# A unit's seventh product behind the next unit's second, rotary tables by residue, and angles once per token and frequency

## The chip, the core and the metric

One core of a Trainium2 chip runs the whole kernel. The metric is the device time in microseconds (us). Engines: TensorE (PE) multiplies, VectorE (DVE) and ScalarE (ACT) work on tiles in SBUF and on the accumulators in PSUM, GpSimd (POOL) on tiles in SBUF, and SyncE (SP) issues all DMAs. Each engine runs its own list of instructions in order. An instruction that waits holds back everything behind it on its engine.

## What is computed

The reference, cut to what the change touches. `h` is the normalised input, 1024 tokens by 1024 features; all is float32.

```python
z = h @ w_in[l]                        # 7696 columns; 1536 of them d_q, 1536 d_k
gates = jax.nn.sigmoid(h @ w_gate[l] + b_gate[l])          # 3072 columns

def rope(x, pos):                      # on d_q and d_k, head size 128
    inv = ROPE_THETA ** (-jnp.arange(0, hd, 2, dtype=jnp.float32) / hd)
    ang = pos.astype(jnp.float32)[..., None] * inv         # 64 frequencies
    cos = jnp.cos(ang)[:, :, None, None, :]
    sin = jnp.sin(ang)[:, :, None, None, :]
    x1, x2 = xf[..., :hd // 2], xf[..., hd // 2:]
    return jnp.concatenate([x1 * cos - x2 * sin, x2 * cos + x1 * sin], axis=-1)
# then three groups of heads attend with dilation 1, 4 and 16: the tokens of one
# residue modulo the dilation make a sequence of their own
```

## The kernel before

**Units.** The projections by `w_in` and `w_gate` are done in units of 256 output columns by 1024 tokens, each a call of `seven`. Channels lie on the partitions, tokens along the free axis. A unit's result is 2x2 blocks of 128x512, and seven block products give it instead of eight. Every float32 operand is split in a high and a low part (`split`: an ACT copy, line 160, and a DVE subtraction, line 161), so a product is four contraction blocks times three matmuls, 12 matmuls of 128x128 by 512. A unit has 84. A unit has three PSUM accumulators. In PE order the products go to X, Y, Z, X, Z, X and X; here they are called product 1 to 7. ACT copies products 1, 3 and 4 out of PSUM (lines 316, 321, 324), DVE adds products 2, 5 and 6 to those copies (lines 318, 327, 329). Products 4, 6 and 7 go on accumulating in X and product 5 in Z, so product 5 cannot begin before line 321 has read Z, product 6 not before line 324 has read X, and product 7 not before line 329 has read X.

**Product 7** is put off: `seven` leaves it in `pending`, and the next unit calls `last_product()` right behind its own product 1 (line 314). Its result, block (1,0), is handed to `use` in PSUM.

**Operands.** A unit's seven weight operands lie in two sets of tiles, operands 1 to 4 in the first and 5 to 7 in the second. The same two sets serve the next unit: its operands 1 to 4 can be written when product 4 is done, its operands 5 to 7 when product 7 is done. The raw weights come by two DMAs of 512 KB into a pool of three `raw` buffers. POOL makes the sums of weight blocks (lines 293 to 299).

**Rotary units.** Between 233 us and 675 us run 22 units: one gate unit (columns 8 and 9 of `w_gate`), 12 rotary ones (`rope_out`: d_q and d_k in turn, four per dilation) mixed with 7 further gate units, and two of `gla_out`. Written T and L (light, a gate unit), the mix is L T L T T L T T L T L T T L T T L T T. For each of its four blocks a rotary unit has ACT copy the two halves of the partitions crosswise into `sw` (lines 519, 520), DVE multiply the block by the cosine (line 526), POOL multiply `sw` by the sine (line 527), and DVE add (line 528). The result is sent to `d_qk` by a DMA. For dilations 4 and 16 lines 526 and 528 read by `perm`, with a stride of 4 or 16 elements, and write the tokens in order of residues.

**Angles.** Lines 488 to 509 make the tables `cos` and `sin`, 128 partitions by 1024 tokens. The 64 frequencies stand twice on the partitions. 16 DVE instructions reduce the angle to -pi to pi, three ACT instructions take the sine.

**Order.** The code is written in the order of the units. A list scheduler lays out each engine's list at compile time, with semaphores for every dependence.

Of the kernel before, what the change touches and what calls it, by code (L numbers as in the profile page):

```python
# [9 lines left out]
F32 = mybir.dt.float32  # L10
F32R = mybir.dt.float32r
I32 = mybir.dt.int32
U8 = mybir.dt.uint8
AF = mybir.ActivationFunctionType
OP = mybir.AluOpType

T = 1024
# [55 lines left out]
def trunk(ctx: ExitStack, tc, x, positions, w_in, w_alpha_up, b_alpha, gla_norm_g, sc_conv_w,  # L73
          w_gate, b_gate, w_branch, w_mix_out, pre_mix_g, post_mix_g, pre_ffn_g, post_ffn_g,
          w_ff_gate, w_ff_up, ff_conv_w, ff_conv_b, w_ff_down, const, masks, out):
    nc = tc.nc
    V, S, G, PE = nc.vector, nc.scalar, nc.gpsimd, nc.tensor

    main = ctx.enter_context(tc.tile_pool(name="main", bufs=1))
    rawp = ctx.enter_context(tc.tile_pool(name="raw", bufs=3))  # L80
# [5 lines left out]
    def pt(tag, name):  # L86
        return psum.tile([128, 512], F32, name=name, tag=tag,
                         bufs={"g": 4, "s": 2, "t": 1, "o": 1}[tag])
# [176 lines left out]
            split(*out(2), f12)  # L265
            split(*out(3), t4)

    def seven(src, c0, B, Ts, tmp, dst, use):


        v = src.rearrange("(k p) c -> p k c", p=128)
        r0, r1 = wload([v[:, :4, c0:c0 + 256], v[:, 4:, c0:c0 + 256]], [8, 256])
# [7 lines left out]
        op = lambda i: ops[i]  # L280
# [25 lines left out]
        def prod(ps, a, b, first):  # L306
            for k in range(4):
                for n, (x, y) in enumerate(((0, 0), (0, 1), (1, 0))):
                    PE.matmul(ps, a[x][:, k], b[y][:, k], start=first and k == 0 and n == 0,  # L309
                              stop=k == 3 and n == 2, skip_group_check=not first)  # L310

        X, Y, Z = pt("g", "sX"), pt("s", "sY"), pt("g", "sZ")
        prod(X, op(0), blk(0, 0), True)
        last_product()
        c11 = dst(0, 0)
        S.activation(c11, X, AF.Copy)
        prod(Y, op(1), blk(1, 0), True)
        sums_taken[1] = V.tensor_tensor(c11, c11, Y, op=OP.add)
        prod(Z, op(2), tt(0), True)
        c22 = dst(1, 1)  # L320
        sums_taken[2] = S.activation(c22, Z, AF.Copy)
        prod(X, op(3), tt(1), False)
        c12 = dst(0, 1)
        sums_taken[3] = S.activation(c12, X, AF.Copy)
        use(0, 0, c11)
        prod(Z, op(4), blk(1, 1), False)
        sums_taken[4] = V.tensor_tensor(c12, c12, Z, op=OP.add)
        prod(X, op(5), tt(2), False)
        sums_taken[5] = V.tensor_tensor(c22, c22, X, op=OP.add)  # L329
        use(0, 1, c12)  # L330
        use(1, 1, c22)

# [3 lines left out]
        pending.append(rest)  # L336


    pending = []

    sops, sums_taken = [], {}

    def op_places():

        ts = [[wp.tile([128, 4, 4, 128], F32R, name=n, tag=n) for n in ("wh", "wl")] for i in range(2)]
        return Ring([(h[:, i], l[:, i]) for h, l in ts for i in range(4)])

    def last_product():
        while pending:
            pending.pop(0)()  # L350
# [134 lines left out]
    last_product()  # L485


    cos, sin = fr[:, 0], fr[:, 1]
    pos = rawp.tile([128, T], I32, name="pos", tag="raw")
    nc.sync.dma_start(pos, bass.AP(tensor=positions.tensor, offset=positions.offset, ap=[[0, 128], [1, T]]))  # L490
    ang, nn = cos, sin
    V.tensor_scalar(ang, pos, cst[:, K_INV:K_INV + 1], None, op0=OP.mult)
    MAGIC = 1.5 * 2.0 ** 23
    V.tensor_scalar(nn, ang, 1.0 / (2.0 * math.pi), MAGIC, op0=OP.mult, op1=OP.add)
# [6 lines left out]
    V.tensor_scalar(nn, ang, -PI, 2.0 * math.pi, op0=OP.is_lt, op1=OP.mult)  # L501
    V.tensor_tensor(ang, ang, nn, op=OP.add)
    V.tensor_scalar(ang, ang, 3.1415925, -3.1415925, op0=OP.min, op1=OP.max)
    ac = fr[:, 2]
    V.scalar_tensor_tensor(ac, ang, -1.0, ang, op0=OP.mult, op1=OP.max)
    V.tensor_scalar(ac, ac, -1.0, math.pi / 2.0, op0=OP.mult, op1=OP.add)
    S.activation(sin[:64], ang[:64], AF.Sin, scale=-1.0)
    S.activation(sin[64:], ang[64:], AF.Sin)
    S.activation(cos, ac, AF.Sin)
    seven(w_gate2, 8 * 128, H, TS, STMP, ring, gate_out(8))  # L510

    DIL = (1, 4, 16)
    SW = Ring([fr[:, 2, :512], fr[:, 2, 512:]])

    def rope_out(w, ch):
        def use(i, l, c):
            hs = slice(l * 512, l * 512 + 512)
            sw = SW()
            S.activation(sw[:64], c[64:], AF.Copy)
            S.activation(sw[64:], c[:64], AF.Copy)  # L520

            d = DIL[ch // 512]
            perm = (lambda x: x) if d == 1 else (lambda x: x.rearrange("p (m r) -> p r m", r=d))
            as_ = (lambda x: x) if d == 1 else (lambda x: x.rearrange("p (r m) -> p r m", r=d))
            o = c if d == 1 and (i, l) != (1, 0) else ring()
            V.tensor_tensor(as_(o), perm(cos[:, hs]), perm(c), op=OP.mult)
            G.tensor_tensor(sw, sw, sin[:, hs], op=OP.mult)  # L527
            V.tensor_tensor(as_(o), as_(o), perm(sw), op=OP.add)  # L528
            r = ch + i * 128
            nc.sync.dma_start(d_qk[w, r:r + 128, hs], o)  # L530
        return use
# [10 lines left out]

    turned = [(w_in2, col + ch, rope_out(w, ch)) for ch in range(0, 1536, 256) for w, col in enumerate((COL_DQ, COL_DK))]
    light = [(w_gate2, dt * 128, gate_out(dt)) for dt in range(10, 24, 2)]
    nt, n = len(turned), len(turned) + len(light)
    for i in range(n):
        take = turned if (i + 1) * nt // n > i * nt // n else light
        src, c0, use = take.pop(0)
        seven(src, c0, H, TS, STMP, ring, use)
    seven(w_in2, COL_GQ, H, TS, STMP, ring, gla_out(0))  # L550
    seven(w_in2, COL_GK, H, TS, STMP, ring, gla_out(1))

# [836 lines left out]
        forms(0, ys, il)  # L1389

    sops.append(op_places())
    sums_taken.clear()
    ring = halves_ring(("t2", "t0", "t1"))
    yring = Ring([fb[:, i] for i in (0, 1, 3)])
# [124 lines left out]
    n = 0  # L1519
# [73 lines left out]
```

## Time and profile before

| what | value |
|---|---|
| median of 3 runs | 1950.78 us (1946.41 to 1953.79) |
| the profiled execution | 1952.54 us, span 1950.8 us |
| PE busy | 1887.3 us of the span |
| DVE, ACT, POOL busy | 1327.7, 876.9, 730.9 us |
| mean granted TensorE clock | 0.988 |
| PE share of the chain that ended last | 77% |

The span is the time from the first to the last instruction of the profile; 1.7 us of the execution lie around it. Times in the rows below count from the span's start. A busy PE is not PE at its peak: its clock has two levels, 2.4 GHz (1.00 in a row) and 1.2 GHz (0.50).

### The profile page before, as it was taken

To read this page: it belongs to the slowest core of one execution; us is meant where nothing else is said; L and a number is where in the kernel's file an instruction comes from. 1 tells how busy PE (TensorE), PEld (TensorE's weight loads), DVE (VectorE), ACT (ScalarE), POOL (GpSimd) and SP (SyncE) were. 2 spreads that over 40 slices of the span, in tenths; PEclk is the share of its full clock that TensorE was granted. 3 is DMA by queue.
4 is the path that set the end of the run, shared out by engine and by line. 5 is a ranking of instruction groups with operands and counts; after the bars stand their busy time and mean duration, and the time that the engine had idled before them with its cause. 6 is when DMAs were issued, how large, how long until landed. Compare 5 with 4: busy or idle time off the path is not lost.

```text
span 1950.8 us, 26312 instructions
## 1 busy us (share of the span) xinstructions
PE 1887.3 (97%) x9649; PEld 1597.8 (82%) x9649; DVE 1327.7 (68%) x1971; ACT 876.9 (45%) x1626; POOL 730.9 (37%) x438
## 2 busy tenths in 40 slices
PE   6999999999999999999999899998999999999998
PEld 5988778888777899899888777886788888888886
DVE  8755675677787543566854577677777777779597
ACT  5433354454444433424546623343443444355453
POOL 4523244555454232102013451016444444526172
PEclk9999999999999999999999999999999999999999
DMA  5122322323232565312467556321323232369863
GB/s 177 66 79 73 123 88 93 123 97 119 97 116 89 184 211 181 135 44 76 127 219 210 173 191 253 108 98 60 103 87 120 96 108 87 125 216 353 275 198 123
DMA packets 192961, 268.32 MB, mean 138 GB/s; under 512 B 30785, under 2 KB 121791, under 8 KB 191808
## 3 DMA queue, kind: packets, MB, share of 16 engines
q1 hardware_dynamic: 192832, 266.64, 40.4%
q8 instruction: 76, 1.25, 0.3%
q14 instruction: 53, 0.43, 0.1%
HBM read 191.73 MB, written 74.86 MB: 137 GB/s over the span
## 4 chain that ended last, share of the span: by engine, by line
PE 77%; DVE 10%; issue 4%; POOL 3%; ACT 3%; DMA 2%; SPq 0%; DVEq 0%; ACTq 0%; POOLq 0%
PE sX L309 24%; PE sZ L309 12%; PE sY L309 6%; PE fX L1537 6%; PE fY L1537 5%; PE vX L604 4%; DVE wl L161 2%; PE vZ L604 2%; PE p L200 1%; PE p L202 1%; PE p L204 1%; PE gs L793 1%; PE mx L1291 1%; PE mx L1293 1%; PE mx L1292 1%
## 5 line engine op out<-in xcount | busy, mean ns | idle before, releaser
L161 DVE TENSOR_TENSOR wl<-raw,wh 128x512 fp32r<-128x512 f32 (+1 forms) x212 | 212.0, 1036 | 103.6 <-ACT wh L160 103.4
L309 PE MATMUL sX<-T,wh 128*128 128x512 f32 x720 | 226.8, 397 | 11.2 <-DVE ring L329 10.5
L160 ACT ACTIVATE wh<-raw 128x512 fp32r<-128x512 f32 (+1 forms) x222 | 142.1, 665 | 79.9 <-PE sX L309 41.2
L309 PEld LDWEIGHTS sX<-T,wh 128*128 128x128 f32 x720 | 136.6, 191 | 44.6 <-DVE ring L329 15.2
L309 PE MATMUL sX<-FT,wh 128*128 128x512 f32 x480 | 149.2, 392 | 3.1 <-DVE ring L329 1.6
L309 PE MATMUL sX<-T,wl 128*128 128x512 f32 x360 | 142.2, 395 | 0.0
L527 POOL TENSOR_TENSOR fr<-fr 128x512 f32<-128x512 f32 x48 | 70.5, 1468 | 148.7 <-ACT fr L520 147.3
L309 PEld LDWEIGHTS sX<-FT,wh 128*128 128x128 f32 x480 | 89.2, 188 | 25.2 <-DVE ring L329 5.4
L161 DVE TENSOR_TENSOR wl<-fr,wh 128x512 fp32r<-128x512 f32 x90 | 65.9, 754 | 63.2 <-ACT wh L160 62.5
L160 ACT ACTIVATE wh<-fr 128x512 fp32r<-128x512 f32 (+1 forms) x99 | 63.9, 665 | 70.1 <-PE sX L309 49.1
L309 PE MATMUL sX<-FT,wl 128*128 128x512 f32 x240 | 93.5, 390 | 0.0
L293 POOL TENSOR_TENSOR fr<-raw 128x512 f32<-128x512 f32 x30 | 41.2, 1374 | 121.9 <-DMA raw<-in_w_gate_dram 45.7
L161 DVE TENSOR_TENSOR ops<-rw,ops 128x512 fp32r<-128x512 f32 x72 | 67.0, 960 | 26.2 <-ACT ops L160 25.0
L299 POOL TENSOR_TENSOR raw<-raw 128x512 f32<-128x512 f32 x50 | 80.9, 1618 | 0.0
L309 PEld LDWEIGHTS sX<-T,wl 128*128 128x128 f32 x360 | 68.8, 191 | 14.7
L1358 POOL TENSOR_TENSOR fb<-fb 128x512 f32<-128x512 f32 x40 | 64.1, 1602 | 42.7 <-DVE fb L1407 31.0
L528 DVE TENSOR_TENSOR ring<-ring,fr 128x512 f32<-128x512 f32 x48 | 56.2, 1172 | 29.7 <-POOL fr L527 28.1
L309 PE MATMUL sZ<-T,wh 128*128 128x512 f32 x240 | 73.9, 389 | 0.0
L1537 PE MATMUL fX<-ops 128*128 128x512 f32 x312 | 73.2, 389 | 0.0
L1537 PEld LDWEIGHTS fX<-ops 128*128 128x128 f32 x312 | 58.6, 188 | 12.1
L297 POOL TENSOR_TENSOR fr<-raw,fr 128x512 f32<-128x512 f32 x30 | 49.7, 1656 | 48.4 <-DVE wl L161 48.4
L160 ACT ACTIVATE ops<-rw 128x512 fp32r<-128x512 f32 x72 | 43.6, 628 | 52.4 <-PE fX L1537 23.6
(550 smaller groups left out, 5596.1 us busy)
## 6 DMA issues: line engine op xcount, KB each, us to landing
rw<-in_w_ff_down_dram SPq DMA_DIRECT2D x99, 256.0 KB
raw<-in_w_in_dram SPq DMA_DIRECT2D x48, 512.0 KB
rw<-d_fa SPq DMA_DIRECT2D x77, 256.0 KB
d_fa<-fb SPq DMA_DIRECT2D x70, 256.0 KB
raw<-in_w_gate_dram SPq DMA_DIRECT2D x24, 512.0 KB
d_sig<-ring SPq DMA_DIRECT2D x48, 256.0 KB
d_qk<-ring SPq DMA_DIRECT2D x48, 256.0 KB
raw<-in_w_ff_gate_dram SPq DMA_DIRECT2D x22, 512.0 KB
```

Source lines behind the costliest of these rows:

```text
L160: S.activation(h, src, AF.Copy)
L161: eng.tensor_tensor(l, src, h.bitcast(F32), op=OP.subtract)
L200: PE.matmul(ps[h], a, xs[h][0][:, kx, :], start=st, stop=False)
L293: G.tensor_tensor(s1, A21, A22, op=OP.add)
L297: G.tensor_tensor(s1, A12, s2, op=OP.subtract)
L299: G.tensor_tensor(A21, A11, A21, op=OP.subtract)
L309: PE.matmul(ps, a[x][:, k], b[y][:, k], start=first and k == 0 and n == 0, stop=k == 3 and n == 2, skip_group_check=not first)
L527: G.tensor_tensor(sw, sw, sin[:, hs], op=OP.mult)
L528: V.tensor_tensor(as_(o), as_(o), perm(sw), op=OP.add)
L604: PE.matmul(o, b[y][:, k, ts], a[:, x, k], start=first and t % 2 == 0 and k == 0 and n == 0, stop=k == 3 and n == 2, skip_group_check=not ...
L1358: G.tensor_tensor(o, p, q, op=op)
L1537: PE.matmul(P[t], o[:, a, ts], o[:, b], start=st, stop=c + k == NCH - 1 and x == 2, skip_group_check=i not in (2, 1, 5))
```

## The change

Three parts, all in the stretch of the rotary units.

1. From the angles on (`slack` is set there and cleared ahead of the feed-forward layer) a unit calls `last_product()` behind its own product 2 instead of product 1.
2. The tables are made half as wide: frequencies times 512 tokens, the first half of the tokens on partitions 0 to 63, the second on 64 to 127. ACT takes sine and cosine in eight instructions of 64x512. The scratch lies in `fr[:, 2]`, where it lay in the tables before.
3. For dilations 4 and 16 the order by residues is made where blocks leave PSUM: the copies and additions of `seven` read PSUM with the stride and write the block in order, and so do the instructions on block (1,0) in `rope_out`. The tables are put in the same order by `tables_by`, once ahead of each dilation, in two further `raw` buffers (6 ACT instructions for dilation 4, 18 for dilation 16). Lines 526 and 528 then read without a stride, and the product with the cosine is written back in place. The mix of units is L T T L T T three times and an L.

```diff
@@ -265,7 +265,8 @@
-    def seven(src, c0, B, Ts, tmp, dst, use):
+    def seven(src, c0, B, Ts, tmp, dst, use, d=1):
...
@@ -309,24 +310,28 @@
+        perm = (lambda a: a) if d == 1 else (lambda a: a.rearrange("p (m r) -> p r m", r=d))
+        as_ = (lambda a: a) if d == 1 else (lambda a: a.rearrange("p (r m) -> p r m", r=d))
         X, Y, Z = pt("g", "sX"), pt("s", "sY"), pt("g", "sZ")
         prod(X, op(0), blk(0, 0), True)
+        if not slack:
+            last_product()
+        c11 = dst(0, 0)
+        S.activation(as_(c11), perm(X), AF.Copy)
+        prod(Y, op(1), blk(1, 0), True)
         last_product()
-        c11 = dst(0, 0)
-        S.activation(c11, X, AF.Copy)
-        prod(Y, op(1), blk(1, 0), True)
-        sums_taken[1] = V.tensor_tensor(c11, c11, Y, op=OP.add)
+        sums_taken[1] = V.tensor_tensor(as_(c11), as_(c11), perm(Y), op=OP.add)
         prod(Z, op(2), tt(0), True)
         c22 = dst(1, 1)
-        sums_taken[2] = S.activation(c22, Z, AF.Copy)
+        sums_taken[2] = S.activation(as_(c22), perm(Z), AF.Copy)
         prod(X, op(3), tt(1), False)
         c12 = dst(0, 1)
-        sums_taken[3] = S.activation(c12, X, AF.Copy)
+        sums_taken[3] = S.activation(as_(c12), perm(X), AF.Copy)
         use(0, 0, c11)
         prod(Z, op(4), blk(1, 1), False)
-        sums_taken[4] = V.tensor_tensor(c12, c12, Z, op=OP.add)
+        sums_taken[4] = V.tensor_tensor(as_(c12), as_(c12), perm(Z), op=OP.add)
         prod(X, op(5), tt(2), False)
-        sums_taken[5] = V.tensor_tensor(c22, c22, X, op=OP.add)
+        sums_taken[5] = V.tensor_tensor(as_(c22), as_(c22), perm(X), op=OP.add)
         use(0, 1, c12)
         use(1, 1, c22)
 
@@ -336,7 +341,7 @@
         pending.append(rest)
 
 
-    pending = []
+    pending, slack = [], []
 
     sops, sums_taken = [], {}
 
@@ -485,10 +490,14 @@
     last_product()
 
 
+    slack.append(True)
     cos, sin = fr[:, 0], fr[:, 1]
-    pos = rawp.tile([128, T], I32, name="pos", tag="raw")
-    nc.sync.dma_start(pos, bass.AP(tensor=positions.tensor, offset=positions.offset, ap=[[0, 128], [1, T]]))
-    ang, nn = cos, sin
+    pos = rawp.tile([128, 512], I32, name="pos", tag="raw")
+    for l in range(2):
+        nc.sync.dma_start(pos[l * 64:l * 64 + 64],
+                          bass.AP(tensor=positions.tensor, offset=positions.offset + 512 * l, ap=[[0, 64], [1, 512]]))
+    ang, nn = fr[:, 2, :512], fr[:, 2, 512:]
     V.tensor_scalar(ang, pos, cst[:, K_INV:K_INV + 1], None, op0=OP.mult)
...
@@ -501,31 +510,53 @@
...
-    ac = fr[:, 2]
+    ac = nn
     V.scalar_tensor_tensor(ac, ang, -1.0, ang, op0=OP.mult, op1=OP.max)
     V.tensor_scalar(ac, ac, -1.0, math.pi / 2.0, op0=OP.mult, op1=OP.add)
-    S.activation(sin[:64], ang[:64], AF.Sin, scale=-1.0)
-    S.activation(sin[64:], ang[64:], AF.Sin)
-    S.activation(cos, ac, AF.Sin)
+    for l in range(2):
+        ps_, hs = slice(l * 64, l * 64 + 64), slice(l * 512, l * 512 + 512)
+        S.activation(sin[:64, hs], ang[ps_], AF.Sin, scale=-1.0)
+        S.activation(sin[64:, hs], ang[ps_], AF.Sin)
+        S.activation(cos[:64, hs], ac[ps_], AF.Sin)
+        S.activation(cos[64:, hs], ac[ps_], AF.Sin)
     seven(w_gate2, 8 * 128, H, TS, STMP, ring, gate_out(8))
 
     DIL = (1, 4, 16)
     SW = Ring([fr[:, 2, :512], fr[:, 2, 512:]])
 
+    def tables_by(d, before):
+        for t in (cos, sin):
+            raw = rawp.tile([128, T], F32, name="tab", tag="raw")
+            for l in range(2):
+                hs = slice(l * 512, l * 512 + 512)
+                n, a = 512 // d, d // before
+                src = t[:, hs].rearrange("p (r0 m r1) -> p r1 r0 m", r0=before, r1=a)
+                o = raw[:, hs].rearrange("p (r1 r0 m) -> p r1 r0 m", r1=a, r0=before)
+                if before == 1:
+                    src, o = src[:, :, 0], o[:, :, 0]
+                    S.activation(o, src, AF.Copy)
+                else:
+                    for r in range(a):
+                        S.activation(o[:, r], src[:, r], AF.Copy)
+            S.activation(t, raw, AF.Copy)
     def rope_out(w, ch):
+        d = DIL[ch // 512]
         def use(i, l, c):
             hs = slice(l * 512, l * 512 + 512)
             sw = SW()
-            S.activation(sw[:64], c[64:], AF.Copy)
-            S.activation(sw[64:], c[:64], AF.Copy)
-
-            d = DIL[ch // 512]
-            perm = (lambda x: x) if d == 1 else (lambda x: x.rearrange("p (m r) -> p r m", r=d))
-            as_ = (lambda x: x) if d == 1 else (lambda x: x.rearrange("p (r m) -> p r m", r=d))
-            o = c if d == 1 and (i, l) != (1, 0) else ring()
-            V.tensor_tensor(as_(o), perm(cos[:, hs]), perm(c), op=OP.mult)
+            perm = (lambda x: x) if d == 1 or (i, l) != (1, 0) else (lambda x: x.rearrange("p (m r) -> p r m", r=d))
+            as_ = (lambda x: x) if d == 1 or (i, l) != (1, 0) else (lambda x: x.rearrange("p (r m) -> p r m", r=d))
+            S.activation(as_(sw[:64]), perm(c[64:]), AF.Copy)
+            S.activation(as_(sw[64:]), perm(c[:64]), AF.Copy)
+            o = c if (i, l) != (1, 0) else ring()
+            V.tensor_tensor(as_(o), as_(cos[:, hs]), perm(c), op=OP.mult)
             G.tensor_tensor(sw, sw, sin[:, hs], op=OP.mult)
-            V.tensor_tensor(as_(o), as_(o), perm(sw), op=OP.add)
+            V.tensor_tensor(o, o, sw, op=OP.add)
             r = ch + i * 128
             nc.sync.dma_start(d_qk[w, r:r + 128, hs], o)
         return use
@@ -542,11 +573,16 @@
 
     turned = [(w_in2, col + ch, rope_out(w, ch)) for ch in range(0, 1536, 256) for w, col in enumerate((COL_DQ, COL_DK))]
     light = [(w_gate2, dt * 128, gate_out(dt)) for dt in range(10, 24, 2)]
-    nt, n = len(turned), len(turned) + len(light)
-    for i in range(n):
-        take = turned if (i + 1) * nt // n > i * nt // n else light
+    for what in "LTTLTT" * 3 + "L":
+        take = turned if what == "T" else light
+        d = 1
+        if what == "T":
+            g = (12 - len(turned)) // 4
+            d = DIL[g]
+            if g and len(turned) % 4 == 0:
+                tables_by(d, DIL[g - 1])
         src, c0, use = take.pop(0)
-        seven(src, c0, H, TS, STMP, ring, use)
+        seven(src, c0, H, TS, STMP, ring, use, d)
     seven(w_in2, COL_GQ, H, TS, STMP, ring, gla_out(0))
     seven(w_in2, COL_GK, H, TS, STMP, ring, gla_out(1))
 
@@ -1389,6 +1425,7 @@
         forms(0, ys, il)
 
     sops.append(op_places())
+    slack.clear()
     sums_taken.clear()
     ring = halves_ring(("t2", "t0", "t1"))
     yring = Ring([fb[:, i] for i in (0, 1, 3)])
```

The order on two engines. First PE, in the first rotary unit, where product 7 of the light unit ahead of it begins: `sX` and `sY` are accumulators, `H0h`, `H0l` and `T3` what is multiplied, `wh` and `wl` the operands. Before:

```order
L309 MATMUL sX_2132<-H0h_96,wh_2110 128x512
L309 MATMUL sX_2132<-H0l_97,wh_2110 128x512
L309 MATMUL sX_2132<-H0h_96,wl_2111 128x512
L309 MATMUL sX_2005<-T3_398,wh_1985 128x512 x2
L309 MATMUL sX_2005<-T3_398,wl_1986 128x512
```

Now:

```order
L310 MATMUL sY_2139<-H0h_96,wh_2116 128x512
L310 MATMUL sY_2139<-H0l_97,wh_2116 128x512
L310 MATMUL sY_2139<-H0h_96,wl_2117 128x512
L310 MATMUL sX_2011<-T3_398,wh_1991 128x512 x2
L310 MATMUL sX_2011<-T3_398,wl_1992 128x512
```

The old unit's product 7 (`sX<-T3`) stood directly behind the new unit's product 1 (`sX<-H0h`); now the new unit's product 2 (`sY`) stands ahead of it.

ACT in the gate unit where the sines are taken, before (the unit behind the gate unit of columns 8 and 9; `ring<-sX,cols` is that gate unit's block (1,0)):

```order
L160 ACTIVATE wh<-fr 128x512
L507 ACT_TABLE_LOAD
L507 ACTIVATE fr<-fr 64x1024
L508 ACTIVATE fr<-fr 64x1024
L160 ACTIVATE wh<-raw 128x512
L509 ACTIVATE fr<-fr 128x1024
L160 ACTIVATE wh<-raw 128x512
L449 ACT_TABLE_LOAD
L449 ACTIVATE ring<-sX,cols 128x512
L321 ACTIVATE ring<-sZ 128x512
L449 ACTIVATE ring<-ring,cols 128x512
```

Now (in the gate unit of columns 8 and 9 itself):

```order
L454 ACTIVATE ring<-ring,cols 128x512
L326 ACTIVATE ring<-sZ 128x512
L518 ACT_TABLE_LOAD
L518 ACTIVATE fr<-fr 64x512
L519 ACTIVATE fr<-fr 64x512
L520 ACTIVATE fr<-fr 64x512
L521 ACTIVATE fr<-fr 64x512
L518 ACTIVATE fr<-fr 64x512
L519 ACTIVATE fr<-fr 64x512
L520 ACTIVATE fr<-fr 64x512
L521 ACTIVATE fr<-fr 64x512
L329 ACTIVATE ring<-sX 128x512
```

The sines moved one unit ahead. They stood in front of the copy of product 3 (`ring<-sZ`), and now stand in front of the copy of product 4 (`ring<-sX`, line 329 of the changed code, which was line 324).

ACT in the light unit ahead of the first unit of dilation 4, behind the copies for `rope_out` of block (1,0) of the unit ahead (`fr<-sX`). A light unit at the same place in the mix before:

```order
L519 ACTIVATE fr<-sX 64x512
L520 ACTIVATE fr<-sX 64x512
L449 ACTIVATE ring<-ring,cols 128x512
L321 ACTIVATE ring<-sZ 128x512
L160 ACTIVATE wh<-raw 128x512
L324 ACTIVATE ring<-sX 128x512
```

Now:

```order
L554 ACTIVATE fr<-sX 64x512
L555 ACTIVATE fr<-sX 64x512
L539 ACTIVATE tab<-fr 128x512
L326 ACTIVATE ring<-sZ 128x512
L543 ACTIVATE fr<-tab 128x1024
L539 ACTIVATE tab<-fr 128x512
L543 ACTIVATE fr<-tab 128x1024
L329 ACTIVATE ring<-sX 128x512
L160 ACTIVATE wh<-raw 128x512 x2
```

Five instructions of `tables_by` stand around the copies of product 3 and product 4.

## Rows read from the trace of the kernel before

**Rows 1.** The page, part 1: busy us of an engine (share of the span), instructions.

```profile
PE 1887.3 (97%) x9649; PEld 1597.8 (82%) x9649; DVE 1327.7 (68%) x1971; ACT 876.9 (45%) x1626; POOL 730.9 (37%) x438
```

**Rows 2.** Waits of PE, 225 to 700 us: us in total, times, longest us.

```profile
PE sX L309 <- DVE ring L329: 10.5, 7, 2.1
PE sZ L309 <- ACT ring L321: 2.8, 1, 2.8
```

**Rows 3.** PE in order of time: start, length, operation; in brackets the idle time before, releaser.

```profile
232.71 0.74 PE L309 MATMUL sX<-T,wh 128*128 128x512 f32 x2 [2.10 <-DVE ring L329]
...
268.93 0.50 PE L309 MATMUL sZ<-H1h,wh 128*128 128x512 f32 x1 [2.77 <-ACT ring L321]
...
356.62 0.73 PE L309 MATMUL sX<-T,wh 128*128 128x512 f32 x2 [0.81 <-DVE ring L329]
...
512.11 0.68 PE L309 MATMUL sX<-T,wh 128*128 128x512 f32 x1 [1.96 <-DVE ring L329]
```

**Rows 4.** Windows: length; busy us (x) of PE, PEld, DVE, ACT, POOL; TensorE clock; DMA; GB/s.

```profile
232.90:236.30 3.40, 3.40 (x16) 2.75 (x16) 0.98 (x2) 0.67 (x2) 0.00 (x0) 1.00 0.40 154
269.92:273.33 3.41, 3.41 (x9) 2.64 (x9) 2.80 (x2) 2.24 (x5) 3.33 (x3) 0.50 0.64 234
512.27:515.67 3.40, 3.40 (x9) 2.63 (x10) 2.94 (x2) 1.14 (x2) 1.90 (x2) 0.50 0.20 77
...
635.15:638.55 3.40, 3.40 (x10) 2.62 (x9) 3.29 (x3) 0.79 (x3) 1.47 (x1) 0.50 0.20 77
```

**Rows 5.** DVE in order of time, end of the second of two dilated rotary units.

```profile
504.67 3.50 DVE L161 TENSOR_TENSOR wl<-raw,wh 128x512 fp32r<-128x512 f32 x2
...
509.30 0.67 DVE L327 TENSOR_TENSOR ring<-ring,sZ 128x512 f32<-128x512 f32 x1
...
511.37 0.69 DVE L329 TENSOR_TENSOR ring<-ring,sX 128x512 f32<-128x512 f32 x1
```

**Rows 6.** DVE in order of time, the same place with dilation 1.

```profile
355.28 0.69 DVE L526 TENSOR_TENSOR ring<-fr,ring 128x512 f32<-128x512 f32 x1 [1.41 <-ACT fr L520]
355.89 0.68 DVE L329 TENSOR_TENSOR ring<-ring,sX 128x512 f32<-128x512 f32 x1
```

**Rows 7.** DVE, line 526 on block (1,0): dilation 1, then dilation 4.

```profile
342.31 0.69 DVE L526 TENSOR_TENSOR ring<-fr,sX 128x512 f32<-128x512 f32 x1
...
421.96 1.08 DVE L526 TENSOR_TENSOR ring<-fr,sX 128x512 f32<-128x512 f32 x1 [0.16 <-ACT fr L520]
```

**Rows 8.** ACT by line: ns of one (min/median/max), first and last start, forms.

```profile
L1010 ACT ACTIVATE dD<-po x8: 572/576/598, 1006.1 to 1118.7; 128x512 f32<-128x512 f32 x8
...
L1013 ACT ACTIVATE dD<-po x8: 1049/1076/1102, 1018.6 to 1101.5; 128x512 f32<-128x512 f32 x8
...
L519 ACT ACTIVATE fr<-ring x36: 628/631/634, 285.2 to 634.5; 64x512 f32<-64x512 f32 x36
...
L872 ACT ACTIVATE gv<-go x32: 268/277/294, 948.5 to 969.1; 128x128 f32<-128x128 f32 x32
```

**Rows 9.** ACT in order of time, where the sines are taken.

```profile
262.14 1.06 ACT L507 ACTIVATE fr<-fr 64x1024 f32<-64x1024 f32 x1
...
266.41 1.28 ACT L449 ACT_TABLE_LOAD   x1
...
268.29 0.59 ACT L321 ACTIVATE ring<-sZ 128x512 f32<-128x512 f32 x1
```

**Rows 10.** PE in order of time: first matmuls of products 5 and 6, gate unit of columns 8 and 9.

```profile
245.57 0.39 PE L309 MATMUL sZ<-H1h,wh 128*128 128x512 f32 x1
...
248.29 0.62 PE L309 MATMUL sX<-T,wh 128*128 128x512 f32 x2
```

**Rows 11.** ACT, copy of product 3 in that unit; then DVE, angles; then POOL.

```profile
243.05 0.60 ACT L321 ACTIVATE ring<-sZ 128x512 f32<-128x512 f32 x1 [1.20 <-PE sZ L309]
...
241.73 7.93 DVE L497 SCALAR_TENSOR_TENSOR fr<-fr 128x1024 f32<-128x1024 f32 x4
...
242.74 1.36 POOL L293 TENSOR_TENSOR fr<-raw 128x512 f32<-128x512 f32 x1 [11.24 <-DMA raw<-in_w_gate_dram]
```

## The prediction

> **What bounds the kernel now.** I read the page's busy shares first: PE works 97% of the span [rows 1], so time can come only from what PE loses. PE's waits were next, and the stretch of the rotary units, which alone the change touches, has two kinds [rows 2]. Product 7 waited seven times, 10.5 us together, for line 329, the addition that reads X before product 7 may write it. Product 5 waited once, 2.8 us, for line 321, the copy of product 3 [rows 2, 3]. Third, the granted clock: after the waits at 269, 512, 573 and 635 us it stands at 0.50 for 3.41 us each (three of the four alike windows are shown). PE starts 9 or 10 matmuls there, against 16 in such a window at 1.00, so each costs about half its length, 1.7 us [rows 4]. The first wait of 2.10 us was followed by no such window [rows 3, 4], so a wait of two microseconds costs a window often, not always.
>
> Why line 329 is late: a product lasts 248.29 - 245.57 = 2.72 us [rows 10], and one product stands between products 6 and 7 as cover. At 512.11 us product 7 was due 1.96 us earlier, at 510.15, so product 6 had ended at 507.43. Line 329 ended at 512.06, 4.6 us behind it, because DVE was still at operand splits and at line 327 long after product 5 [rows 5]. In the pair with dilation 1 the due time was 355.81, product 6 ended at 353.09 and line 329 at 356.57, 3.5 us later [rows 3, 6]. The waits come where the second of two rotary units ends, and once behind the angles; the first of the seven, 2.10 us, is where the code asks for product 7 directly behind product 6, ahead of the angles. That place stays.
>
> **Part 1, product 7 behind product 2.** No instruction is added. The cover grows from 2.72 to 5.44 us. Line 329, 3.5 to 4.6 us late, then ends before product 7 is due, with 0.8 to 1.9 us left. That removes 10.5 - 2.1 = 8.4 us of waits and three windows at half clock, 3 x 1.7 = 5.1 us. What it defers: operands 5 to 7 of the new unit go into tiles that product 7 frees, now 8.2 us into the unit instead of 5.4, and product 5 needs operand 5 at 13.6. One ACT split (0.63) and a DVE subtraction behind the work in the queue lie between; I count 11 to 13 us, so this costs nothing, but the cover is 1 to 3 us. Block (1,0) itself leaves 2.72 us later, with two copies on ACT, two instructions on DVE, one on POOL and a DMA on SP. A weight load behind that DMA comes later by as much; POOL once waited 11.24 us for such a load without a wait of PE behind it [rows 11], so I take nothing for it.
>
> **Part 2, angles.** The positions come by two DMAs instead of one, tens of microseconds ahead. The DVE chain is halved in width and starts earlier, since its scratch is free once an earlier block has been sent. Before, ACT took two table loads and three sines in front of line 321 [rows 9], and that was the 2.8 us wait, with its window 4.5 us. These go. In their place, by the order, eight sines of 64x512 stand between the copies of products 3 and 4 of the gate unit. Product 3's copy ended at 243.65 [rows 11], the table load is 1.28 [rows 9], and eight instructions at the 0.63 of a 64x512 copy [rows 8] are 5.0: 243.65 + 1.28 + 5.0 = 249.9, and the copy of product 4 ends near 250.5. Product 6 is due at 248.29 [rows 10]: a new wait of 2.2 us. If the sines start back to back, about 0.54 apart, it is 1.5. If the DVE chain is late it is up to 4.0: four of its 1024-wide steps took 7.93 us while POOL began on operands at 242.74 beside them [rows 11], and the halved chain ends beside the same POOL instructions. I take 2.5, and a half-clock window behind it, 1.7, as behind three of the four waits of that size.
>
> **Part 3, order by residues.** DVE gains: with dilation 1 line 526 takes 0.69 us on block (1,0), with dilation 4 1.08 [rows 7]. Two instructions on each of four blocks lose that factor. DVE pays some back: three additions per unit now read PSUM with a stride. No row shows a strided PSUM read with nothing else strided; the bounds are 0.69 and 1.08 on DVE, and on ACT 0.58 and 1.08, the copy in order and the copy with a strided write [rows 8]. I take the middle. And line 526 now writes in place for all dilations, so it must wait for ACT's two crosswise copies, as it does for dilation 1: 1.41 us of idle DVE [rows 6]. So DVE's relief is largely used up: line 329 should end about 4 to 6 us behind product 6, against a cover of 5.4.
>
> In the second unit of each dilated pair (four of them) I count from the unit's start: first addition over at 7.7, ACT's two crosswise copies (1.3) to 9.0, three operand splits to 10.7, two copies out of PSUM for the old block (1,0), then the copy of product 3. At 0.60 each it is over at 12.5, at 1.08 at 13.9; product 5 is due at 13.6. So 0 to 0.3 us here and 0 to 0.4 at product 7: four times 0 to 0.7, 0 to 2.8; I take 1.0.
>
> The tables turn twice, in a light unit. Behind the crosswise copies of the old block, which end 11 to 13 us into it, ACT has strided copies of 512 (0.63 to 1.08) or of 128 elements (0.28 [rows 8], or about 0.4), and two copies back of 1024, taken at the 1.06 us of a 1024-wide sine [rows 9], the first of them waiting until DVE has read the old cosine. The copy of product 4 then ends at 17.0 to 17.5, where product 6 is due at 16.3; for dilation 16 product 5 waits up to 1.3 and product 6 0.4 to 1.0. Together 0 to 4.5; I take 2.4. The two further `raw` buffers hold back a weight load of the next unit until the first table is copied back; its operand is needed 5 us after that at the earliest, and the upper end includes what it may cost.
>
> [...]
>
> **Sum.** Removed: 8.4 + 2.8 + 4 x 1.7 = 18.0 us. Added: 2.5 + 1.7 (sines), 2.4 (tables), 1.0 (second units) = 7.6. Net 10.4 us. The execution profiled took 1952.54, so 1942.1; it lies 1.8 above the median of the runs, so **1940.4 us**. Ends: all costs at their lowest 18.0 - 1.5 = 16.5, giving 1934.3; all at their highest 18.0 - 4.0 - 1.7 - 4.5 - 2.8 = 5.0, giving 1945.8.
>
> **Rivals.** *Strided PSUM is free.* For it: ACT reads PSUM no slower than SBUF in order [rows 8]. Tables and second units then cost 1 us together: net 18.0 - 4.2 - 1.0 = 12.8, and with short sines and no window up to 16.5: 1934 to 1938.
>
> *Strided PSUM at its upper ends, or product 7 still late.* For it: 1.08 on a strided block [rows 7, 8], and the in-place wait [rows 6]. Net 18.0 - 4.2 - 4.5 - 2.8 = 6.5: 1944.3. If the addition also comes 6.2 us behind product 6, product 7 still waits 0.8 at four places, 3.2 more: 1947.5. Then part 1 does only in part what it says. [...]
>
> *Slower.* ACT becomes the bound in the second dilated units. If a strided copy out of PSUM takes 2.2 us rather than 1.08, the copies ahead of product 5 (of product 1, two crosswise, of product 3) end 4 x 1.1 = 4.4 us later, product 5 waits 4.7, and the clock falls each time: 4 x (4.7 + 1.7) = 25.6. Net -18.0 + 7.6 + 25.6 - 1.0 = +14: 1965. It turns slower than before where these waits pass 2 us and cost a window each, 4 x 3.7 = 14.8 against the 11.4 left, with some 1.5 us a copy. Against it: no copy of 512 on ACT takes more than 1.10 in the rows [rows 8].
>
> **How the numbers follow.** Forecast (net 8 to 13) 0.50; free strides (over 13, up to 16.5) 0.16; upper ends (2 to 8) 0.28; slower 0.06. A measurement of this kernel tells 0.5%, 9.8 us, from no change, and the forecast lies just beyond that. Two thirds of the forecast's chance, 0.34, and all of the free strides give faster, 0.50; the rest of the forecast and the upper ends 0.44; slower 0.06. The range leaves out the slower case and the tails of the two others: 1934 to 1948.
>
> **What would show it.** Right: line 329's successor releases no idle PE between 250 and 660 us, and the windows at 0.50 there fall from four to one. One new wait stands near 248 us, of product 6 for the copy of product 4 behind the sines, 1.5 to 4 us. DVE's instructions of the rotary block take 0.69 with every dilation. Copies and additions out of PSUM tell which end holds, 0.6 or 1.08. Two light units, ahead of dilations 4 and 16, show waits of about 1 us on those copies. Wrong: waits of product 5 in the second units of dilated pairs, or a second window at half clock there. Everything behind the rotary units keeps its order but for small shifts in the value projections, where PE doesn't wait today; a wait there would be outside the sum.

## The result, and the profile after

The changed kernel is slower: 1980.68 us (1977.78 to 1981.45, 4 runs) against 1951.99 (1946.41 to 1953.79, 4 runs), a ratio of 1.0154 with a 95% interval of 1.0138 to 1.0170. The prediction, 1940.4 with 1934 to 1948, was wrong in sign and outside its range.

In the changed code the matmuls are line 310, the copies of products 1, 3 and 4 are lines 320, 326 and 329, and the additions of products 2, 5 and 6 lines 323, 332 and 334. The page of the profiled run (span 1976.0), part 1, beside [rows 1]:

```profile
PE 1889.8 (96%) x9649; PEld 1596.1 (81%) x9649; DVE 1290.0 (65%) x1971; ACT 895.2 (45%) x1655; POOL 738.0 (37%) x438
```

DVE was relieved as expected, 1290.0 against 1327.7 us, and it brought nothing. The loss lies wholly in the rotary units and the value projections behind them: the first matmul after these, `up`, starts at 832.72 us against 803.74, 29.0 later, and the span is 25.2 longer. PE's waits from 225 to 720 us (us in total, times, longest), which answer to [rows 2]:

```profile
PE sZ L310 <- ACT ring L326: 13.5, 9, 4.6
PE sX L310 <- DVE ring L334: 13.4, 7, 2.8
PE sX L310 <- ACT ring L329: 5.9, 2, 4.8
```

Before, product 7 waited 10.5 us and product 5 2.8. The deferral was to leave product 7 only the first of its seven waits, and there are seven again (line 334 is the line 329 of before); product 5 now waits nine times for the copy of product 3. PE in order of time, the places that tell the causes apart (as [rows 3]):

```profile
253.70 1.22 PE L310 MATMUL sX<-T,wh 128*128 128x512 f32 x2 [4.78 <-ACT ring L329]
...
312.02 0.50 PE L310 MATMUL sZ<-H1h,wh 128*128 128x512 f32 x1 [1.05 <-ACT ring L326]
325.56 0.73 PE L310 MATMUL sX<-T,wh 128*128 128x512 f32 x2 [2.37 <-DVE ring L334]
...
377.37 0.80 PE L310 MATMUL sZ<-H1h,wh 128*128 128x512 f32 x1 [4.58 <-ACT ring L326]
...
504.67 0.78 PE L310 MATMUL sZ<-H1h,wh 128*128 128x512 f32 x1 [4.15 <-ACT ring L326]
...
752.91 6.02 PE L640 MATMUL vZ<-wl,T 128*128 128x256 f32 x48 [1.54 <-ACT vout L645]
```

253.70 is product 6 behind the sines; 312.02 product 5 in a second rotary unit, 325.56 product 7 of that unit; 377.37 and 504.67 product 5 where the tables turn; 752.91 a value projection. Windows at half clock, columns as in [rows 4]:

```profile
252.15:258.96 6.81, 5.25 (x12) 4.13 (x13) 1.95 (x3) 5.66 (x9) 0.00 (x0) 0.50 0.10 39
375.03:381.84 6.81, 4.47 (x11) 3.51 (x12) 4.45 (x7) 4.76 (x7) 2.80 (x2) 0.50 0.35 116
453.53:456.93 3.40, 3.40 (x10) 2.62 (x9) 1.99 (x4) 0.78 (x3) 1.79 (x1) 0.50 0.23 82
504.73:508.13 3.40, 3.40 (x8) 2.73 (x9) 1.05 (x2) 3.33 (x9) 1.11 (x1) 0.50 0.53 191
579.83:583.23 3.40, 2.91 (x7) 2.33 (x8) 1.82 (x3) 1.85 (x3) 2.55 (x2) 0.50 0.20 77
```

They cover 23.9 us, but three of them begin before a wait of PE is over, and only where PE works does the clock cost time: half of PE's 19.4 busy us in them, 9.7, against 6.8 before. By place: sines 4.78 + 2.6 (window) = 7.4; turns 4.58 + 2.2 + 4.15 + 1.7 = 12.6; six waits of product 7 10.75 + 3.2 = 13.9; product 5 in second units and in the light units behind them 4.8; value projections 3.7; a product 6 in the last unit 1.1; the first wait of 2.64, which stood there before with 2.10. That is 46 against 13.3 + 6.8 = 20.1 before: 26 of the 29 us. (The expectations below take half of each whole window and so have 8.2, 13.8 and 14.2 for the first three.)

**Where the lateness comes from.** One second rotary unit, which begins at 297.09 us. SP, ACT and DVE in it, three lists:

```profile
313.37 0.38 SPq L171 DMA_DIRECT2D raw<-in_w_gate_dram  x1
```

```profile
307.13 0.63 ACT L554 ACTIVATE fr<-ring 64x512 f32<-64x512 f32 x1 [2.67 <-DVE ring L323]
307.78 0.63 ACT L555 ACTIVATE fr<-ring 64x512 f32<-64x512 f32 x1
308.44 0.63 ACT L160 ACTIVATE wh<-fr 128x512 fp32r<-128x512 f32 x1
308.98 1.13 ACT L160 ACTIVATE wh<-raw 128x512 fp32r<-128x512 f32 x2
...
316.88 0.63 ACT L160 ACTIVATE wh<-raw 128x512 fp32r<-128x512 f32 x1 [3.90 <-DMA raw<-in_w_gate_dram]
```

```profile
306.35 0.68 DVE L323 TENSOR_TENSOR ring<-ring,sY 128x512 f32<-128x512 f32 x1
...
311.54 2.38 DVE L161 TENSOR_TENSOR wl<-raw,wh 128x512 fp32r<-128x512 f32 x2
...
322.14 0.68 DVE L332 TENSOR_TENSOR ring<-ring,sZ 128x512 f32<-128x512 f32 x1
...
324.83 0.68 DVE L334 TENSOR_TENSOR ring<-ring,sX 128x512 f32<-128x512 f32 x1
```

Product 7 of the unit ahead ends near 305.4. ACT could then split operands 5 to 7, which read `raw` for the last time, but the crosswise copies of this unit's first block now stand ahead of them and wait for line 323. DVE's half follows at 311.54, and only then is a `raw` buffer free: SP, which had sent the block ahead of the load in its list at 311.04 and then waited 2.0 us more for DVE's split, issues the second half of the next unit's weights at 313.37, 16.3 us into the unit. ACT goes on with it at 316.88, after 3.90 us of waiting; the splits of operands 1 to 4, POOL's sums and, behind them on DVE, lines 332 and 334 come later with it. In the kernel before, in the second unit of the first pair of rotary units, the same place, which begins at 333.56, the same half is issued 8.1 us into the unit:

```profile
341.65 0.38 SPq L171 DMA_DIRECT2D raw<-in_w_gate_dram  x1
```

So I had two explanations to tell apart. *Loads*: buffers come free late, loads land late, everything behind them is late. *Order*: the copies and splits in front of line 334 and line 326 are too many or wrongly ordered on ACT and DVE, and the loads are only late beside it.

### The profile page after: what moved, and what is told of

It reads as the page before. It is cut to its first block, busy times and chain, and to the rows that moved or that the text cites. A ratio compares the mean times of both kernels' runs of the same rounds, so it can differ in the third digit from the quotient of the medians.

```text
span 1976.0 us, 26372 instructions
## 1 busy us (share of the span) xinstructions
PE 1889.8 (96%) x9649; PEld 1596.1 (81%) x9649; DVE 1290.0 (65%) x1971; ACT 895.2 (45%) x1655; POOL 738.0 (37%) x438
## 4 chain that ended last, share of the span: by engine, by line
PE 64%; DVE 13%; POOL 6%; DMA 6%; issue 6%; ACT 5%; SPq 0%; DVEq 0%; ACTq 0%; POOLq 0%
PE sX L310 20%; PE sZ L310 10%; PE fX L1574 6%; PE sY L310 5%; PE fY L1574 5%; DVE wl L161 3%; PE vX L640 2%; DMA d_mw<-mws 1%; POOL fr L558 1%; DMA mws<-in_w_mix_out_dram 1%; PE gs L829 1%; PE p L200 1%; PE mx L1329 1%; PE mx L1327 1%; PE mx L1328 1%
## 5 line engine op out<-in xcount | busy, mean ns | idle before, releaser
L161 DVE TENSOR_TENSOR wl<-raw,wh 128x512 fp32r<-128x512 f32 (+1 forms) x212 | 200.9, 977 | 126.5 <-ACT wh L160 126.5
L161 DVE TENSOR_TENSOR wl<-fr,wh 128x512 fp32r<-128x512 f32 x90 | 98.3, 1100 | 41.1 <-ACT wh L160 38.4
L558 POOL TENSOR_TENSOR fr<-fr 128x512 f32<-128x512 f32 x48 | 80.4, 1675 | 101.6 <-ACT fr L555 101.6
L294 POOL TENSOR_TENSOR fb<-raw 128x512 f32<-128x512 f32 x20 | 27.3, 1363 | 94.7 <-DVE fb L1381 22.4
L310 PE MATMUL sZ<-H1h,wh 128*128 128x512 f32 x120 | 49.5, 412 | 13.5 <-ACT ring L326 13.5
```

Of the source, the lines that this page charges most:

```text
L161: eng.tensor_tensor(l, src, h.bitcast(F32), op=OP.subtract)
L294: G.tensor_tensor(s1, A21, A22, op=OP.add)
```

## The experiments

All ratios are to the kernel before, run on the same chip beside each experiment; experiments on different chips are compared by their ratios.

**Part 1 alone.** The kernel before with

```diff
-        last_product()
+        if not slack:
+            last_product()
         ...
         prod(Y, op(1), blk(1, 0), True)
+        last_product()
```

> The kernel before with part 1 alone (product 7 runs behind the next unit's second product; order, angles and mix as before). As the prediction had it: the six waits of 1.40 us and most of the half-clock windows go, the cover of 5.44 us holds in every unit, and the time is 1937 to 1944 us (before 1952). Theory of the weight loads: the later splits of operands 5 to 7 hold back the raw buffers, the next unit's weight load is issued and lands some 8 us later in the second unit of each pair, its operands and sums come late, product 7 waits there anyway for 2.4 to 2.8 us in six units, with its windows: about 8.4 + 6.8 us removed and 10 to 14 us back, 1947 to 1953 us. Theory of the engines' order (copies of product 1 and 2 across the rows ahead of the splits on ScalarE, no load late): the same waits, but the loads land no later after the start of a unit than before (about 11 us).

Measured: 1964.12 us, ratio 1.0079 (1.0061 to 1.0098). The deferral by itself costs some 15 us, more than either theory had. Waits for a `raw` load, 265 to 720 us (us in total, times, longest):

```profile
ACT wh L160 <- DMA raw<-in_w_gate_dram: 15.6, 6, 4.9
ACT wh L160 <- DMA raw<-in_w_in_dram: 13.5, 13, 2.5
```

ACT waited for a load 19 times, 29.1 us; in the kernel before not once in that stretch. The load shown above is issued here at 348.62 us, 16.0 us into the unit that begins at 332.65. PE, 225 to 720 us (line 323 is here the copy of product 3, line 331 the addition of product 6):

```profile
PE sZ L309 <- ACT ring L323: 15.6, 12, 3.5
PE sX L309 <- DVE ring L331: 8.0, 5, 2.3
```

Product 7's waits fell only from 10.5 to 8.0, and twelve waits of product 5 came. That the loads are late speaks for the first theory; it does not yet show that they are the cause.

**Part 1 undone**, the rest of the change kept: the line `slack.append(True)` is left out.

> The changed kernel without part 1 (product 7 again behind the next unit's first product; order by residues, angles by token and the new mix stay). Theory of the weight loads: product 7 waits its 1.40 us in the second units again, operands are split as early as before, loads land some 11 us after a unit's start, the products 5 no longer wait for product 3's copy in the second units; sines (8.2 us with their windows) and tables (13.8 us) stay. Removed: 14.2 + 4.8 us of waits and windows of product 7 and product 5, back: up to 8.4 + 6.8 us: 1972 to 1980 us. Theory of the engines' order: the copies in the second units are late with or without part 1, and the waits of product 5 stay: 1980 to 1986 us.

Measured: 1950.44 us, ratio 1.0016 (1.0001 to 1.0031). Without the deferral 1.4% go, some 27 us, where I had expected 1 to 9, and the two turns of the tables no longer stop PE. From 225 to 720 us:

```profile
PE sX L310 <- DVE ring L334: 8.7, 8, 2.6
PE sX L310 <- ACT ring L329: 4.2, 1, 4.2
```

The waits of product 5 in the second units went as well, against what the theory of the order had. So the 12.6 us at the turns, which I had put down to part 3, were the deferral's. After, the first copy of a turn waited for its buffer (ACT, columns as above):

```profile
375.71 1.12 ACT L539 ACTIVATE tab<-fr 128x512 f32<-128x512 f32 x1 [2.58 <-DVE wl L161]
376.73 0.58 ACT L326 ACTIVATE ring<-sZ 128x512 f32<-128x512 f32 x1
```

Line 539 stands ahead of line 326, the copy that product 5 needs, and waits for a `raw` buffer that the late splits still hold. (375.71 lies in the second rotary unit ahead of the light unit; the instructions of `tables_by` that stand under "The change" as a light unit's are these.)

**A fourth `raw` buffer.** The deferral stays; the units and the tables take their buffers from a ring of four, the fourth being a third of the staging ring:

```diff
+    ring = halves_ring(("t0", "t1"))
+    rawq.append(Ring([rawp.tile([128, 4, 256], F32, name="raw", tag="raw") for i in range(3)]
+                     + [slot("t2", [128, 4, 256], name="raw")]))
```

> The changed kernel with a fourth buffer for weight loads and tables in the rotary stretch (taken out of the staging ring, which has four halves left there in place of six). Theory of the weight loads: loads are issued as early as in the kernel before, the waits of product 7 in the second units shrink from 2.4-2.8 us to under 0.7 us with their windows (12 us gained), the first table of a light unit no longer waits for a buffer (product 5's waits of 4.58 and 4.15 us fall to about 3): 1962 to 1970 us. Theory of the engines' order: loads land earlier and the splits run no earlier: within 4 us of 1980.

Measured: 1943.26 us, ratio 0.9970 (0.9959 to 0.9982): 1.8% below the changed kernel, some 36 us, more than expected. The waits of PE, 225 to 720 us (lines are 5 higher here: 331 is line 326 of the changed kernel, 334 line 329, 339 line 334):

```profile
PE sX L315 <- ACT ring L334: 5.3, 2, 4.2
PE sX L315 <- DVE ring L339: 2.6, 1, 2.6
PE sZ L315 <- ACT ring L331: 2.3, 2, 1.5
```

Of product 7's seven waits only the first, at 231.62 us, is left, and the turns wait 1.05 and 1.54. Waits for a load, 265 to 720 us, are gone but for

```profile
ACT wh L160 <- DMA raw<-in_w_in_dram: 0.4, 2, 0.2
```

The same second unit begins at 295.72 here. SP, which now issues that load in the unit ahead of it, then ACT and DVE in it:

```profile
289.97 0.38 SPq L276 DMA_DIRECT2D raw<-in_w_gate_dram  x1
```

```profile
302.42 0.63 ACT L562 ACTIVATE fr<-ring 64x512 f32<-64x512 f32 x1 [2.67 <-DVE ring L328]
303.07 0.63 ACT L563 ACTIVATE fr<-ring 64x512 f32<-64x512 f32 x1
303.85 0.64 ACT L160 ACTIVATE wh<-fr 128x512 fp32r<-128x512 f32 x1
...
309.29 0.63 ACT L160 ACTIVATE wh<-raw 128x512 fp32r<-128x512 f32 x1 [1.89 <-PE sX L315]
...
310.31 0.62 ACT L160 ACTIVATE wh<-raw 128x512 fp32r<-128x512 f32 x1
```

```profile
301.65 0.68 DVE L328 TENSOR_TENSOR ring<-ring,sY 128x512 f32<-128x512 f32 x1
...
318.61 0.68 DVE L339 TENSOR_TENSOR ring<-ring,sX 128x512 f32<-128x512 f32 x1
```

The crosswise copies stand ahead of the splits as they did, with the same idle 2.67 us for the same addition. But operands 1 and 2 of the next unit are split at 13.6 and 14.6 us of this one, the first held by product 4 alone, where operand 2 had waited for its load until 19.8; and the addition of product 6 starts 22.9 us into the unit and not 27.7. ACT's list in this unit has the same order of copies and splits as far as operand 2, so this decides for the loads, against the order.

**The ring cut, without the buffer.** Three buffers, staging ring of four halves: `ring = halves_ring(("t0", "t1"))` alone.

> The changed kernel with three weight buffers and the staging ring cut to four halves, as in the run with the fourth buffer: what that run did beside the buffer. Theory of the weight loads: the gain of 37 us there came from the buffer alone, and this is 1977 to 1986 us. If the shorter ring was what helped (another order of stores and loads in SP's queue): below 1965 us.

Measured: 1977.06 us, ratio 1.0148 (1.0132 to 1.0164), as the changed kernel. The gain was the buffer's, not the shorter ring's. (The run with four buffers also takes the three old ones from a fixed ring instead of the pool; that by itself was not tried.)

**Four buffers, part 1 undone.**

> The fourth weight buffer with product 7 behind the first product again (part 1 undone), the last corner of a square: three or four buffers, with or without the deferral; three buffers without it gave 1950.4, with it 1980.7, four with it 1943.3. If the buffers only have to make up for the deferral (theory of the weight loads): without it the loads were already in time (1.4 us of waits for a load, against 27.4 with it), a fourth buffer changes nothing, and product 7's waits of 0.8 to 1.6 us stay: 1947 to 1951 us, so that the deferral is worth 4 to 8 us where the buffers allow it. If a fourth buffer is a gain of its own, which would be had without the deferral: 1940 to 1945 us.

Measured: 1943.65 us, ratio 0.9974 (0.9960 to 0.9988). The square, as ratios:

| | product 7 behind product 1 | behind product 2 |
|---|---|---|
| three buffers | 1.0016 | 1.0154 |
| four buffers | 0.9974 | 0.9970 |

My first branch fails, the second holds: the fourth buffer is a gain without the deferral too, 0.4% or some 8 us, and the deferral on top of it is worth nothing that can be measured. With three buffers and no deferral ACT hardly waits for loads, but POOL does; the same row with three buffers, then with four:

```profile
POOL fr L294 <- DMA raw<-in_w_in_dram: 28.8, 6, 11.7
```

```profile
POOL fr L299 <- DMA raw<-in_w_in_dram: 8.6, 2, 4.4
```

And PE's waits for the addition of product 6 fall from 8.7 us to

```profile
PE sX L315 <- DVE ring L339: 3.3, 2, 2.9
```

of which 2.88 are the first wait, ahead of the rotary units; without it 6.1 us became 0.4. So in this kernel the waits of product 7, which the deferral was made to hide, came from buffers too. For the kernel before that is not shown: a fourth buffer was not tried there, and its trace speaks against it, since from 265 to 720 us POOL waited for a `raw` load for 1.8 us in the operand sums and 1.4 us ahead of a product with the sine, against the 28.8 us above.

**The old mix** of light and rotary units in the changed kernel.

> The changed kernel with the order of light and rotary units of before (LTLTTLTTLTLTTLTTLTT in place of LTTLTT three times and L). Theory of the weight loads: fewer second rotary units directly behind a first one make no great difference, six pairs stay six pairs: 1976 to 1984 us. Theory that the new mix is what hurts (tables in the second rotary unit ahead of a light unit, and value projections that wait): tables of a whole sequence come behind other units, and 5 us or more go: 1966 to 1975 us.

Measured: 1971.07 us, ratio 1.0117 (1.0098 to 1.0136): the new mix costs some 7 us with three buffers. The waits for line 326 fall from 13.5 to 8.4 us, and one of 6.18 us on an operand's split comes (409.17 us). Which feature of the mix it is stays open.

**The sines behind the copy of product 4**, four buffers: the eight activations are emitted behind the gate unit, not before that copy.

> Four weight buffers, and the eight sines behind the copy of product 4 on ScalarE in place of ahead of it. The run with four buffers still waits 4.22 us there and has a half-clock window of 6.83 us behind it. If the sines are what holds that copy: 4.2 + 3.4 = 7.6 us go, 1935 to 1938 us. If product 4's copy was late for another reason, or the sines now hold up the next copies instead (the table loads, the rotary unit that reads them): 1940 to 1944 us.

Measured: 1941.35 us, ratio 0.9961 (0.9951 to 0.9972), not to be told from the 0.9970 with the sines in front. The wait of 4.22 for that copy went and another came, at the second product of the next unit:

```profile
260.96 0.50 PE L315 MATMUL sY<-H0h,wh 128*128 128x512 f32 x1 [3.59 <-ACT wh L160]
```

On ACT sines and sigmoids alternate there, so function tables were loaded over and over, 1.28 us each (250.41, 252.45, 254.39, 256.43 us). With the turns of the tables put behind product 4's copies as well:

> The same with the tables' turns by residues also behind a copy of product 4. With four buffers the waits at the two turns are 1.05 and 1.54 us; if it is the turn's copies ahead of product 3's or 4's copy on ScalarE, 1.5 to 2.6 us more go than in the run with the sines alone (1933 to 1936 us); if the turns then hold up the rotary copies, no difference or 1 to 3 us more.

Measured: 1943.60 us, ratio 0.9975 (0.9962 to 0.9987). No gain: 1.29 and 1.44 us of waits for operands replace the 1.05 and 1.54.

**The angles one unit earlier**, four buffers: scratch in `fr[:, 1]`, which the convolution has done with, the sine's table in `fr[:, 2]`.

```diff
+        if jp:
+            ang, ac = angles()
         seven(w_in2, COL_SB + 256 * jp, H, TS, STMP, ring, use_b)
```

> Four weight buffers, and the chain of angles one unit earlier (its scratch in the quarter that the shift convolution has done with, sine's table in the other), so that the eight sines stand among ScalarE's copies of the unit before the gate unit and ahead of no copy of product 4 there. If it is the late sines that cost 4.22 us and the half-clock window of 6.83 us in the run with four buffers: these go and 0 to 2 us come back from the sines in the unit before, 1935 to 1940 us. If the sines cost the same wherever they stand on ScalarE (as in the run in which they stood behind product 4's copy and 3.59 us came back at the next unit's operands): 1941 to 1945 us.

> The same with product 7 behind the first product (part 1 undone). The runs with four buffers, with and without the deferral, gave 1943.3 and 1943.7 us. If the deferral is worth nothing once the loads are in time: within 2 us of the run with early angles and the deferral. If it is worth the 1.4 us of cover for each unit in which the sums come late: 3 to 6 us more than that run.

Measured: with the deferral 1940.65 us, ratio 0.9949 (0.9932 to 0.9965); without it 1939.10, 0.9948 (0.9929 to 0.9966). No wait and no half-clock window at the sines is left. One unit earlier, where the chain on DVE now lies, product 7 waits 1.86 us instead, at 215.88, with 3.41 us at half clock (without the deferral 1.85 us at 214.68 and no window); the first wait, 2.56 us with four buffers, is gone. Once more the deferral makes no difference. These two beat both kernels, the one before by 10 to 11 us.

**The same with three buffers and no deferral.**

> Early angles with three weight buffers and no deferral: parts 2 and 3 of the change alone, with the sines out of the way. If the fourth buffer gave the 7 us between 1950.4 and 1943.7 because product 7's waits (eight, 8.7 us) come from loads that land late: those stay, and only the sines' 4.2 + 1.7 us go, 1943 to 1946 us, some 5 us above the run with four buffers.

Measured: 1947.05 us, ratio 0.9979 (0.9966 to 0.9992). Without the fourth buffer and the deferral, angles and order by residues gain 4 us; the waits for line 334 stay, 9.3 us with the first one, which lies at 216.79 here, and the buffer is worth 6 us more, near the 8 of the square.

## Why the prediction was wrong

**The step that failed** is in part 1. I counted product 7's cover (5.44 us) against a line 329 that would come 3.5 to 4.6, at most 6.2 us behind product 6, as if nothing upstream moved. I named what moves, "A weight load behind that DMA comes later by as much", and wrote "so I take nothing for it", because POOL had waited 11.24 us for a load without a wait of PE [rows 11]. The load does not come later by 2.72 us but by 8.2 (16.3 against 8.1 us into a unit), and not because of that DMA: the splits of operands 5 to 7 must come before `raw` is free, and they slipped behind line 323's wait on ACT. So the addition of product 6 came some 5 us later: 27.7 us into the unit, against 22.3 in the kernel before (355.89 [rows 6], in the unit from 333.56) and 22.9 with four buffers. It ended 7.8 to 8.2 us behind product 6 at four of the six places (the wait and the cover of 5.44), not 3.5 to 4.6; the cover was used up, and the 8.4 us of waits that were to go became 10.75 us. Part 1, taken as a gain of 13.5 us with the load at nothing, cost some 27 us (1.0154 against 1.0016 without it). The rest of the sum nearly held: for parts 2 and 3 without part 1 it has 4.5 us removed and 7.6 added, and they measured 0.16%, some 3 us, slower. That is in part luck, since its terms were off: the sines cost 4.17 us and a window there, the turns nothing.

**Product 5's operand** ("I count 11 to 13 us, so this costs nothing") held nearly: one wait of 0.9 us for a split in the run with part 1 alone. But product 5 also needs the copy of product 3, on the same ACT, and that copy comes behind copies that wait for additions that come late. In the unit shown the first addition was over at 9.9 us, where I had counted 7.7 and where it is 6.6 with four buffers; the copies and splits behind it took about what I had counted. The term "0 to 2.8; I take 1.0" was 4.8 for this, the light units behind included, and 13.9 for product 7 in all six pairs.

**Tables**: taken 2.4, at most 4.5, measured 12.6 with the windows. The place was misread: the first copy of a turn stands in the second rotary unit ahead of the light unit, in front of the copy of product 3. I had put the buffer's price at the next unit's load; it fell on the turn's own copy. With four buffers both turns together wait 2.6 us with no window, near the number taken.

**Sines**: place and releaser right (product 6 on the copy of product 4), size not: 4.78 us for 2.5, above the upper end of 4.0, and a window of 6.83 us for one of 3.41, 7.4 for 4.2. The chain on DVE was late, the case named for that end: ACT's first sine started at 247.05, idle 1.63 us for it, and another 0.88 us ahead of the third.

**Strides** out of PSUM cost nothing, the premise of the rival with 0.16. ACT, then DVE by line, 230 to 720 us (busy us, mean ns; idle ahead), all reading PSUM:

```profile
L326 ACT ACTIVATE ring<-sZ 128x512 f32<-128x512 f32 x22 | 13.1, 596 | 5.4 <-PE sZ L310 5.1
...
L554 ACT ACTIVATE fr<-sX 64x512 f32<-64x512 f32 x12 | 7.2, 596 | 0.3
```

```profile
L557 DVE TENSOR_TENSOR ring<-fr,sX 128x512 f32<-128x512 f32 x12 | 8.2, 681 | 2.3 <-ACT fr L555 2.3
```

596 ns and 681 against the 0.58 to 0.60 and 0.69 us of a copy and an addition in order [rows 7, 8]; a stride of 4 or 16 is in eight of the twelve of lines 554 and 557 and in eight of the 22 of line 326, and the longest of each took 597, 689 and 603 ns. The Trainium skill ("SBUF — State Buffer", section "Door 1: The DMA port swizzle") gives PSUM lines of 8 bytes and says of matmuls that access to PSUM which is not contiguous slows them; it does not say so of ACT and DVE, and these reads show no such cost. The slower rival, ACT bound by copies of 2.2 us, foresaw places, product 5 in second units and, where the tables turn, half clock with it, but by a mechanism that did not occur.

**The warning** that "a wait there would be outside the sum" for the value projections came true with 3.7 us.

## What to carry to other kernels

Before moving work later, list the buffers whose release it holds and follow each to the load that waits for it: here a load that slipped 8 us took some 27 us, where the waits and windows that the move was to remove came to 13.5. Where an engine's sums come late, ask first whether its inputs came late, by the waits for loads of all engines, those of the engines far from the bound too. With three buffers the new order of the products lost 27 us and with four it gained nothing; one buffer more was worth 36 us with it and 8 without.

## What the runs showed of the hardware

- Reading PSUM with a stride of 4 or 16 elements cost ACT and DVE nothing at 512 float32 columns (the rows above). Reading SBUF with a stride of 4 did cost ACT: the turn's copies take 1115 ns for 512 columns, against 0.62 to 0.64 us of a split's copy of as many in order (line 160 above).

```profile
L539 ACT ACTIVATE tab<-fr 128x512 f32<-128x512 f32 x4 | 4.5, 1115 | 2.6 <-DVE wl L161 2.6
```

- With a wait of 4.78 or 4.58 us came 6.83 us at half clock, which began 1.6 and 2.3 us before the wait was over, and with one of 4.15 us 3.41. Of the shorter waits of 2.4 to 2.8 us two (2.54 at 452.34, 2.77 at 580.32) came with 3.41 us and three (2.64 at 233.21, 2.37 at 325.56, 2.46 at 642.85) with none: a price per wait can be given only as a mean.
